# First attention: the softmax denominators' reciprocals turned once per unit, and multiplied with the gates in eight 32-row operations

## The chip, the cores and the metric

The kernel runs on one core of a Trainium2 chip. A core has five engines that run side by side: TensorE (PE, matrix products into PSUM; PEld is its loading of the stationary operand), VectorE (DVE), ScalarE (ACT), GpSimd (POOL) and SyncE (SP, which here starts most transfers). Each runs its own queue of instructions in order; semaphores hold an instruction until what it needs is there. SBUF is the memory that all read and write, PSUM (8 banks of 128x512 float32) is where PE writes. The metric is the device time of one execution in microseconds (us), the median of several runs. Engine times of single instructions are in nanoseconds (ns) where marked.

## The reference

Two layers over 256 context tokens and 1024 latent tokens of width 1024. The first is windowed attention with grouped heads and sink logits, the second latent attention. The change lies in the first: 16 heads of 64, in 4 groups that share keys and values; a block of 128 latent queries sees its own block of keys, the one before, the one behind, and the 256 context keys; a context query sees the context alone.

```
def softmax_with_sink(s, sink):
    sk = jnp.broadcast_to(sink, s.shape[:-1] + (1,))
    p = jax.nn.softmax(jnp.concatenate([s, sk], axis=-1), axis=-1)
    return p[..., :-1]
...
        p = softmax_with_sink(jnp.concatenate([s_loc, s_ctx], axis=-1), sink_b).astype(v.dtype)
        return (jnp.einsum("bhgqk,bkhd->bqhgd", p[..., :3 * BLOCK], v)
                + jnp.einsum("bhgqc,bchd->bqhgd", p[..., 3 * BLOCK:], vc))
...
    yx = (ox * jax.nn.silu(gx)) @ w_out
```

The kernel does not divide the probabilities. It multiplies the weighted values by 1/denominator and by the gate silu(g) at the end.

## The kernel before

All of it is float32; products that need the precision are split into a high and a low part (`split`, lines 272 and 273: ACT rounds to the high part, DVE or POOL subtracts for the low one) and `mm3` (lines 277 to 279) adds three products.

The first attention runs in 40 units, `UnitA(ti, g)`: a block `ti` of 128 queries (two context blocks and eight latent ones, in the order 2, 0, 3, 1, 4 to 9) and a group `g` of four heads. A unit has `m` chunks of 128 keys: 2 for a context block, 4 for the first and the last latent block, 5 for the others. Its steps:

- `score(h)`: two matmuls for each of one or two key ranges (256 context keys; up to 384 local ones) into one of three banks (`pss3`), then on DVE a fused masking, scaling and running minimum, line 696, which also writes the scores to SBUF and so frees the bank. `exp(h)` on ACT, line 702, sums the denominators.
- `T(ci)`: four transposes on PE, line 719, of the probabilities of a key chunk into a bank of the ring `pst3` (banks 6, 7, 3), then `split` (ACT, DVE) into SBUF. `PV(ci)`: two matmuls, line 729, into bank 5, accumulated over the chunks; the result has 64 + 64 rows (the two halves of the values' split) and, for each of four heads, 128 query columns.
- `post`, `post2` (lines 706 to 714): the sink's term is added to the denominators (128 queries x 4 heads, POOL), DVE takes the reciprocals (line 712), and POOL copies each head's column into 64 columns of `rb` (128x256, line 714).
- `fin`: ACT copies the halves of `PV`'s result to `o` and `o2`, laid out as 64 rows per head, two heads below each other and two side by side (128 x 2 x 128); lines 739, 740.
- `fin2`, issued in the next unit: PE transposes `rb` in two pieces of 128x128 (line 748) into a bank of `pst3`, so that row and head now match `o`. POOL adds `o2` to `o` (751), DVE multiplies the turned reciprocals by the gate `gt` into `rs` (752), POOL multiplies `o` by `rs` (753) and cuts the product in a high and a low part (755, 756) in `og`. For the last unit (`fast`) DVE does POOL's steps too.

After the four units of a block, `outproj` multiplies its `og` by the output weights; its matmuls are spread as a filler over the next block's units. DVE multiplies by the layer's gate (776), POOL adds the residual (777).

The order of instructions is not the order of the text. From the last projections of the first layer to the start of the second attention, every operation is recorded with an estimated duration and then emitted by a list scheduler (`Plan.emit`): for each engine, at the time it becomes free, the ready operation that stands earliest in the text. Its price for a DVE operation that touches PSUM is

```
        return (0.07 if psum else 0.03) + n * 0.00106, 0.37
```

with n the elements per partition, whatever the number of partitions. The banks and ring buffers are given out in the order of the text, before the scheduling.

Of the kernel before, what the change touches and what calls it, by code (L numbers as in the profile page):

```python
# [48 lines left out]
def shp(ap, *dims):  # L49
    n = 1  # L50
    for d in dims:
        n *= d
    ap = ap[:, 0:n]
    if len(dims) == 1:
        return ap
    names = "abcdefg"[: len(dims)]
    kw = {c: d for c, d in zip(names[1:], dims[1:])}
    return ap.rearrange("p (" + " ".join(names) + ") -> p " + " ".join(names), **kw)
# [151 lines left out]
def kernel(ctx: ExitStack, tc: tile.TileContext, t, out, dbg=None):  # L210
    plan = Plan()
    nc = Recorder(tc.nc, plan)
# [6 lines left out]
    F = cpool.tile([128, F_KB * KB], F32, name="arena_f")  # L219
    ident = cpool.tile([128, 128], F32, name="ident")  # L220
# [395 lines left out]
    gc = f_at(48, 1024)  # L616
    ytmp = Ring(F, [12], 512)
    wstg = Ring(F, [4, 6, 12, 34, 36], 512)
    rbr = Ring(F, [42, 47], 256)
    or1, or2, rtr = (Ring(F, [o, o - 5], 256) for o in (43, 44, 45))  # L620
    Pr = Ring(F, [14 + 2.5 * i for i in range(8)], 640)
    gr = Ring(F, [1.5, 2.5, 46], 256)
# [6 lines left out]
    pst3 = Banks(6, 7, 3)  # L629
# [15 lines left out]
    class UnitA:  # L645
# [63 lines left out]
        def post2(self):  # L709
            den = self.den  # L710
            nc.gpsimd.tensor_add(den, den, self.esk)
            nc.vector.reciprocal(den, den)
            self.rb = rbr.next()
            nc.gpsimd.tensor_copy(shp(self.rb, 4, 64), den.unsqueeze(2).to_broadcast([128, 4, 64]))

        def T(self, ci):
            pt = shp(pst3(), 4, 128)
# [25 lines left out]
        def fin2(self, fast=False):  # L743
            g, og = self.g, self.og
            o, o2 = self.o, self.o2
            rt = shp(pst3(), 4, 128)
            for j in range(2):
                nc.tensor.transpose(rt[:, j, :], self.rb[:, j * 128 : j * 128 + 128], ident)  # L748
            rs = shp(rtr.next(), 2, 128)
            eng = nc.vector if fast else nc.gpsimd  # L750
            eng.tensor_add(o, o, o2)
            nc.vector.tensor_mul(rs, rt[:, 0:2, :], self.gt)
            eng.tensor_mul(o, o, rs)
            hi = og[:, 0, 2 * g : 2 * g + 2, :]
            eng.tensor_copy(hi, o)
            eng.tensor_sub(og[:, 1, 2 * g : 2 * g + 2, :], o, hi.bitcast(F32))
# [296 lines left out]
    for bi, gp, c in order:  # L1053
# [20 lines left out]
        r = proj_t(bi, gp, c)  # L1074
# [885 lines left out]
```

## Time and profile before

| | |
|---|---|
| median of 3 runs | 1501.03 us (1500.3 to 1501.78) |
| profiled execution | 1501.05 us |
| its span, first to last instruction | 1499.2 us |
| mean granted TensorE clock | 0.998 |
| line 748 (turn of the reciprocals) | 80 transposes, 272 ns each by the profile |
| line 752 (reciprocals times gates) | 40 operations of 128x256, 421 ns each |
| line 714 (spread of the reciprocals) | 40 copies of 128x256 on POOL, 407 ns each |

How to read the profile: an engine's busy time is the time in which it executes; matmuls overlap each other, so durations of single ones add up to more than PE's time. A group is one line of the program on one engine, with output and input (partitions x elements), count, busy time, mean duration of one, and the idle time just before it with what ended it. A wait names the engine and line that waited, what it waited for, the sum, the number of times, and the longest. A timeline row gives start and duration; "x2" merges neighbours, whose duration then runs from the first one's start to the last one's end. The chain of waits goes back from the last instruction to whatever released it.

### The profile page before, as it was taken

What the parts mean: (1) busy time and instruction counts of PE and PEld (TensorE: products, weight loads), DVE (VectorE), ACT (ScalarE), POOL (GpSimd) and SP (SyncE); (2) the same over time, 40 slices, a digit from 0 to 9 for tenths busy, and PEclk for the clock granted to TensorE, in tenths of its full rate; (3) what the DMA queues carried; (4) which work ended last, traced back from release to release, by engine and by line L of the source; (5) the groups of instructions that cost most, each with busy time, mean ns of one, the idle gap of its engine ahead of it and who ended that gap; (6) DMA issues with size and microseconds to landing.
All of it is one profiled execution on the core that took longest, in us unless ns stands there. A gap on an engine that the chain in (4) does not pass through costs nothing.

```text
span 1499.2 us, 24997 instructions
## 1 busy us (share of the span) xinstructions
PE 1477.8 (99%) x9162; PEld 1201.7 (80%) x9162; DVE 954.7 (64%) x1871; ACT 709.2 (47%) x1363; POOL 820.3 (55%) x739
## 2 busy tenths in 40 slices
PE   6999999999999999999999999999999999999998
PEld 4888888888888888889888888776777767876687
DVE  4787698748778888878354004575566566566744
ACT  4421222369887888875233421453354434443322
POOL 2563365356454444457246510598788788789100
PEclk9999999999999999999999999999999999999999
DMA  9555654664354332343028622302121222121542
GB/s 338 165 175 170 204 169 155 215 205 122 115 159 127 95 102 89 94 125 132 30 85 292 195 68 85 92 15 79 47 60 54 65 59 60 48 62 30 161 148 85
DMA packets 128339, 178.93 MB, mean 119 GB/s; under 512 B 11980, under 2 KB 80716, under 8 KB 128216
## 3 DMA queue, kind: packets, MB, share of 16 engines
q1 hardware_dynamic: 123960, 170.93, 36.5%
q10 hardware_dynamic: 4256, 6.40, 1.2%
q8 instruction: 72, 1.18, 0.3%
q14 instruction: 51, 0.42, 0.1%
HBM read 131.13 MB, written 46.15 MB: 118 GB/s over the span
## 4 chain that ended last, share of the span: by engine, by line
PE 93%; DMA 2%; issue 2%; DVE 1%; POOL 1%; ACT 0%; POOLq 0%; DVEq 0%; SPq 0%; ACTq 0%
PE PB L277 15%; PE PB L278 15%; PE PB L279 15%; PE PB L1657 13%; PE PB L1680 9%; PE PB L729 5%; PE PB L1623 5%; PE PB L719 5%; PE PB L689 3%; PE PB L690 3%; DMA arena_f<-ada_w 1%; PE PB L1691 1%; PE PB L898 1%; PE PB L831 1%; PE PB L748 1%
## 5 line engine op out<-in xcount | busy, mean ns | idle before, releaser
L277 PE MATMUL PB<-arena_r 128*128 128x512 f32 (+2 forms) x1240 | 452.0, 365 | 0.0
L278 PE MATMUL PB<-arena_r 128*128 128x512 f32 (+2 forms) x1240 | 445.9, 360 | 0.4 <-DVE arena_r L273 0.3
L279 PE MATMUL PB<-arena_r 128*128 128x512 f32 (+2 forms) x1240 | 445.4, 359 | 0.0
L1673 POOL TENSOR_TENSOR arena_f<-arena_f 128x1024 f32<-128x1024 f32 x120 | 285.8, 2382 | 8.2
L277 PEld LDWEIGHTS PB<-arena_r 128*128 128x128 f32 x1240 | 233.9, 189 | 44.5 <-issue 9.2
L279 PEld LDWEIGHTS PB<-arena_r 128*128 128x128 f32 x1240 | 233.9, 189 | 34.1
L278 PEld LDWEIGHTS PB<-arena_r 128*128 128x128 f32 x1240 | 234.1, 189 | 32.9 <-DVE arena_r L273 0.7
L1657 PE MATMUL PB<-arena_r 64*128 64x512 f32 (+1 forms) x1600 | 225.8, 394 | 0.0
L1629 DVE TENSOR_REDUCE krF<-PB 128x1 f32<-128x512 f32 (+1 forms) x264 | 167.1, 677 | 78.8 <-PE PB L1623 78.8
L1667 ACT ACTIVATE arena_f<-PB 128x1024 f32<-128x1024 f32 x160 | 164.5, 1028 | 111.4 <-PE PB L1657 83.4
L273 POOL TENSOR_TENSOR arena_r<-arena_f,arena_r 128x512 fp32r<-128x512 f32 (+1 forms) x98 | 132.5, 1366 | 142.9 <-ACT arena_r L272 124.7
L273 DVE TENSOR_TENSOR arena_r<-PB,arena_r 128x512 fp32r<-128x512 f32 (+2 forms) x215 | 139.8, 662 | 76.3 <-ACT arena_r L272 75.4
L1657 PEld LDWEIGHTS PB<-arena_r 64*128 64x128 f32 (+1 forms) x1600 | 175.2, 185 | 15.8 <-issue 5.2
L696 DVE CUSTOM_DVE_ANT_0 arena_f<-PB,arena_f,small 128x256 f32<-128x256 f32 (+1 forms) x288 | 148.1, 524 | 51.4 <-PE PB L690 33.2
L272 ACT CAST arena_r<-PB 128x512 fp32r<-128x512 f32 (+2 forms) x215 | 119.9, 564 | 109.8 <-PE PB L279 73.3
L1680 PE MATMUL PB<-arena_f 128*64 128x512 f32 x640 | 145.9, 595 | 0.0
L702 ACT ACTIVATE arena_f<-arena_f,small 128x640 f32<-128x640 f32 (+2 forms) x160 | 119.1, 745 | 15.5 <-DVE small L696 13.9
L499 DVE SCALAR_TENSOR_TENSOR arena_f<-arena_f,small 128x512 f32<-128x512 f32 x98 | 113.8, 1205 | 9.9 <-DMA arena_f<-ada_w 9.5
L729 PE MATMUL PB<-arena_r 128*128 128x512 f32 x336 | 118.6, 429 | 0.0
L1623 PE MATMUL PB<-arena_r 64*128 64x512 f32 (+1 forms) x768 | 109.4, 354 | 0.0
L719 PE MATMUL PB<-ident,arena_f 128*128 128x128 f32 x672 | 108.6, 272 | 0.1
L1680 PEld LDWEIGHTS PB<-arena_f 128*64 128x64 f32 x640 | 44.0, 137 | 79.6 <-issue 78.7
(178 smaller groups left out, 1934.8 us busy)
## 6 DMA issues: line engine op xcount, KB each, us to landing
arena_f<-ada_w SPq DMA_DIRECT2D x96, 256.0 KB, 4.0
arena_r<-q_d SPq DMA_DIRECT2D x160, 128.0 KB, 2.8
arena_f<-a_w_in SPq DMA_DIRECT2D x40, 256.0 KB, 3.8
arena_f<-x SPq DMA_DIRECT2D x16, 512.0 KB, 6.6
q_d<-arena_f SPq DMA_DIRECT2D x16, 512.0 KB, 3.0
qn_d<-arena_f SPq DMA_DIRECT2D x16, 512.0 KB, 4.7
arena_r<-qn_d SPq DMA_DIRECT2D x16, 512.0 KB, 5.4
arena_f<-b_w_in SPq DMA_DIRECT2D x24, 256.0 KB, 4.7
```

The lines of the kernel that those rows point to most:

```text
L273: (lo_eng or nc.vector).tensor_sub(lo, src, hi.bitcast(F32))
L277: nc.tensor.matmul(o, ah, bh, start=first, stop=False)
L278: nc.tensor.matmul(o, al, bh, start=False, stop=False)
L279: nc.tensor.matmul(o, ah, bl, start=False, stop=last)
L719: nc.tensor.transpose(pt[:, h, :], self.Ps[h][:, ci * 128 : ci * 128 + 128], ident)
L729: nc.tensor.matmul(self.pv, V[:, self.chunks[ci], self.g, :], PT[:, s], start=ci == 0 and s == 0, stop=ci == self.m - 1 and s == 1,)
L1623: nc.tensor.matmul(bank[:, o : o + n], self.q[r, s, bs], k[r, 0, n0 : n0 + n], start=s == 0, stop=s == 2)
L1629: nc.vector.reduce_max(self.mxp[:, e, b : b + 1, i], bank[:, 0:n], AX.X)
L1657: nc.tensor.matmul(PB[:, b + e, :], k[r, s, cs], q[r, sq], start=i == 0, stop=i == 4)
L1667: nc.scalar.activation(E, PB[:, b : b + 2, :], AF.Exp)
L1673: eng.tensor_add(acc, acc, E)
L1680: nc.tensor.matmul(PB[r, 7, :], Vq[:, c, h, :], E[:, e], start=c == 0, stop=c == NT - 1)
```

## The change

`post2` spreads each head's reciprocal over 32 columns, not 64, so `rb` is 128x128 and one transpose turns it. In the turned tile, rows 32h to 32h+31 hold the reciprocals of head h. A head's 64 rows of `rs` are now made in two products of 32 rows, both from those same 32 rows of the turned tile; with four heads that is eight DVE operations of 32 partitions x 128 elements in place of one of 128 x 256. Output and gate start at partition 0, 32, 64, 96 in turn, the turned reciprocals at 32h.

```
@@ -616,7 +616,7 @@
-    rbr = Ring(F, [42, 47], 256)
+    rbr = Ring(F, [42, 47], 128)
@@ -711,7 +711,7 @@
             self.rb = rbr.next()
-            nc.gpsimd.tensor_copy(shp(self.rb, 4, 64), den.unsqueeze(2).to_broadcast([128, 4, 64]))
+            nc.gpsimd.tensor_copy(shp(self.rb, 4, 32), den.unsqueeze(2).to_broadcast([128, 4, 32]))
@@ -743,13 +743,15 @@
             o, o2 = self.o, self.o2
-            rt = shp(pst3(), 4, 128)
-            for j in range(2):
-                nc.tensor.transpose(rt[:, j, :], self.rb[:, j * 128 : j * 128 + 128], ident)
+            rt = pst3()[:, 0:128]
+            nc.tensor.transpose(rt, self.rb, ident)
             rs = shp(rtr.next(), 2, 128)
             eng = nc.vector if fast else nc.gpsimd
             eng.tensor_add(o, o, o2)
-            nc.vector.tensor_mul(rs, rt[:, 0:2, :], self.gt)
+            for h in range(4):
+                for x in range(2):
+                    r = slice(64 * (h % 2) + 32 * x, 64 * (h % 2) + 32 * x + 32)
+                    nc.vector.tensor_mul(rs[r, h // 2], rt[32 * h : 32 * h + 32], self.gt[r, h // 2])
             eng.tensor_mul(o, o, rs)
```

## The prediction

> **What bounds the kernel now.** I read the whole page first, then the stretch in which the changed lines run. Columns of the second fence are the stretch, its length, and the busy time and count of each engine.
>
> ```profile
> span 1499.2 us, 24997 instructions
> PE 1477.8 (99%) x9162; PEld 1201.7 (80%) x9162; DVE 954.7 (64%) x1871; ACT 709.2 (47%) x1363; POOL 820.3 (55%) x739
> ...
> PE   6999999999999999999999999999999999999998
> ...
> DVE  4787698748778888878354004575566566566744
> ...
> L748 PE MATMUL PB<-ident,arena_f x80: 270/272/276, 334.1 to 664.8; 128*128 128x128 f32 x80
> ```
>
> ```profile
> 340.00:655.00 315.00, 315.00 (x1932) 276.89 (x1931) 256.45 (x778) 261.76 (x644) 148.10 (x283) 1.00 0.36 108
> ...
> by line: PE PB L729 22.9%; PE PB L719 21.4%; PE PB L690 11.5%; PE PB L689 11.5%; PE PB L278 10.1%; PE PB L277 10.1%; PE PB L279 10.0%; PE PB L748 2.6%
> ```
>
> TensorE (PE) is busy nearly everywhere, and the last row of the first fence places the change: the turn of the reciprocals, line 748, runs 80 times between 334 and 665 us, in the attention stage (slices 10 to 18, where the DVE digits are 7 and 8, against 64% over the span). Between 340 and 655 us PE has no idle time, its clock is 1.00, and the chain of waits there consists of PE lines alone. DVE has 256 of 315 us, ACT 262, POOL 148. So PE sets the stage, and DVE and ACT are close behind: what counts is how much room DVE has. The waits of DVE in that stretch (total, times, longest) and its groups there:
>
> ```profile
> DVE arena_f L696 <- PE PB L690: 27.9, 44, 2.6
> DVE arena_r L273 <- ACT arena_r L272: 11.1, 24, 1.7
> DVE small L712 <- POOL small L711: 2.6, 4, 0.8
> DVE arena_f L776 <- PE PB L279: 2.5, 7, 0.4
> DVE arena_f L1113 <- POOL small L1109: 1.0, 1, 1.0
> DVE arena_f L752 <- PE PB L719: 0.5, 1, 0.5
> DVE arena_f L696 <- PE PB L719: 0.4, 1, 0.4
> ```
>
> ```profile
> L696 DVE CUSTOM_DVE_ANT_0 arena_f<-PB,arena_f,small 128x384 f32<-128x384 f32 x96 | 59.0, 615 | 9.6
> ...
> L752 DVE TENSOR_TENSOR arena_f<-PB,arena_f 128x256 f32<-128x256 f32 x37 | 15.6, 421 | 0.6 <-PE PB L719 0.5
> ```
>
> The waits sum to 46.0 us. The rest of DVE's idle time (315 - 256.5 - 46.0 = 12.5 us) is short gaps that no engine ends: 9.6 us of it stands before the second score reduction of a head, which needs the running extreme that the first one leaves, and I count it as occupied. So DVE is taken for 315 - 46 = 269 us, with 37 units in the stretch (the count of line 752), and can take 46 / 37 = 1.24 us more per unit before it is full.
>
> **The change part by part.** *PE.* One of two transposes per unit goes. The stretch's chain gives line 748 2.6% of 315 us = 8.2 us for 74 of them, 0.11 us each; 40 fewer are 4.4 us, all on the path as long as PE sets the end.
>
> *DVE.* The one product of 128x256 becomes eight of 32x128. No row shows that shape, so I take duration and pitch (start to next start) from the nearest ones.
>
> ```profile
> L386 DVE TENSOR_TENSOR krF<-PB,arena_f 128x32 f32<-128x32 f32 x8 | 1.4, 170 | 0.0
> L515 DVE TENSOR_TENSOR arena_f<-PB,arena_f 1x512 f32<-1x512 f32 x6 | 4.1, 686 | 15.2 <-PE PB L510 15.1
> L1641 DVE TENSOR_TENSOR arena_r<-PB,ident 4x512 fp32r<-4x512 f32 x32 | 22.1, 690 | 71.0 <-PE PB L1637 70.6
> L273 DVE TENSOR_TENSOR arena_r<-PB,arena_r 128x512 fp32r<-128x512 f32 x156 | 105.2, 685 | 11.5 <-ACT arena_r L272 11.1
> ```
>
> One row, 4 rows and 128 rows of 512 columns all take 686 to 690 ns: fewer rows save nothing. From 256 to 512 columns a product out of PSUM grows by 685 - 421 = 264 ns, 1.03 ns a column, so 128 columns take 421 - 132 = 289 ns (down from 256 towards the 170 ns of 32 columns, the straight line gives 278). The pitch differs between two kinds of neighbours:
>
> ```profile
> 551.58 1.28 DVE L273 TENSOR_TENSOR arena_r<-PB,arena_r 128x512 fp32r<-128x512 f32 x2
> ...
> 558.88 0.42 DVE L752 TENSOR_TENSOR arena_f<-PB,arena_f 128x256 f32<-128x256 f32 x1
> 559.21 0.47 DVE L696 CUSTOM_DVE_ANT_0 arena_f<-PB,arena_f,small 128x256 f32<-128x256 f32 x1
> ...
> 125.61 2.84 DVE L515 TENSOR_TENSOR arena_f<-PB,arena_f 1x512 f32<-1x512 f32 x4 [5.97 <-PE PB L510]
> ...
> 961.22 1.40 DVE L1641 TENSOR_TENSOR arena_r<-PB,ident 4x512 fp32r<-4x512 f32 x2 [3.71 <-PE PB L1637]
> ```
>
> Two subtractions on all 128 partitions take 1.28 us together: the second starts 1.28 - 0.685 = 0.595 us after the first, 0.09 us before that ends. Line 752 shows the same: the next instruction starts 0.33 us after it, though it lasts 0.42. Lines 515 and 1641 step over the partitions, as the new products do (rows 0, 32, 64, 96 at line 515; rows 32 and then 96 at line 1641). There the pitch is (2.84 - 0.686) / 3 = 0.72 us and 1.40 - 0.69 = 0.71: no overlap, and 0.02 to 0.03 us in between. Each of the eight products starts in another group of 32 partitions than the one before it, in its output or in an input, and the instruction behind the eighth starts at partition 0 again. So I take 289 + 30 = 0.32 us each, 2.55 us for the eight against the 0.33 of today: +2.22 us a unit. The other bound is the pitch of aligned neighbours, 289 - 90 = 0.20 us: 1.6 - 0.33 = +1.25 us a unit. I choose the first, since its rows are the ones that shift partitions.
>
> [...]
>
> Over the stretch: 37 x 2.22 = 82 us of new DVE time against 46 us of waits. If every wait were used up, DVE would need 269 + 82 = 351 us where the stage has 315: +36 us, and PE's 4.4 us are worth nothing, since PE then waits for DVE. Some waits stay. Those for PE's scores (27.9 + 0.4 + 0.5) came from PE being the slower one and should vanish; those for ACT's cast, for POOL and for the projection (11.1 + 2.6 + 2.5 + 1.0 = 17.2 us) are the order of other engines' queues. Bounds are none and all of the 17.2; I take half, 8.6, which gives +44.6 us. The other three units lie at the two ends: the opening has waits beside them, and at the closing one, 2.2 us stand on the way to the last output projection, which has other matmuls to run meanwhile. I put the ends at nothing, with 0 to 5 us as the bound.
>
> *What is behind the products.* POOL's line 753 waits for the last product and starts 2.2 us later, and behind it on POOL stand lines 755, 756 and the next unit's denominator (706, 711). The rows of POOL in the stretch:
>
> ```profile
> L753 POOL TENSOR_TENSOR arena_f<-arena_f 128x256 f32<-128x256 f32 x37 | 27.4, 741 | 19.8 <-DVE arena_f L752 19.1
> ...
> L714 POOL COPY arena_f<-small 128x256 f32<-128x256 f32 x38 | 15.5, 408 | 30.3 <-DVE small L712 20.7 <-PE PB L719 6.9 <-DVE small L1108 2.7
> ...
> L706 POOL TENSOR_TENSOR small<-small 128x4 f32<-128x4 f32 x37 | 7.6, 206 | 1.8 <-DVE small L696 1.8
> ```
>
> POOL is idle for more than half of the stretch, and a unit lasts 315 / 37 = 8.5 us, so 2.2 us of lateness does not reach the next unit's turn. The copy at line 714 halves to 128 columns, between 206 ns (4 columns) and 408: it saves at most 0.2 us a unit on POOL, worth nothing under that cover, and up to 0.2 us x 37 = 7.5 us if POOL's cover were gone. The PSUM bank of the turn, one of three shared with the transposes of line 719, is held for 2.55 us instead of 0.42; with DVE the slower engine PE has that time. No DMA is added, moved or removed, and the rings keep their places.
>
> Sum against the profiled execution, 1501.05 us with a span of 1499.2 (1.85 us lie around it; the median of the runs is 1501.03): 1501.05 + 44.6 = 1545.6, so 1546 us.
>
> **The rivals.** *DVE has room and PE stays the bound.* The products pitch at 0.20 us, fall into the 12.5 us of gaps and the waits, and the stage loses its 40 transposes: 1501 - 4.4 = 1497 us. For it: PE alone is on the chain, and 37 x 1.25 = 46 us is not above 46. Against it: it needs the aligned pitch, and every wait used to the last, without PE losing any time.
>
> *DVE is just full.* At 0.20 us DVE needs 269 + 46 = 315 us, the present length, and keeps 0 to 17 us of waits: +0 to +17, at half +9, 1510 us. For it: the aligned pairs. Against it: lines 515 and 1641.
>
> *The products cost more than their own time.* Each one held splits DVE's stream: where the written order puts other instructions between them, these lose their overlap too, 0.09 us for up to eight neighbours, 0.7 us a unit or 27 us, and the bank held longer stops PE's transposes while DVE waits for scores. +44.6 + 27 = +72, 1573 us. It decides where the eight do not run as one block. Against it: they become ready together and follow one another in the code.
>
> *PE is relieved and nothing follows,* within 3 us of before: the lower edge of the second rival, with no wait kept.
>
> **How the numbers follow.** Forecast 0.70, its own range +30 to +62 (1531 to 1563): below, the +36 less part of the short gaps; above, all 17.2 us of waits and 5 us at the ends, with a few interleaved products. First rival 0.07; DVE just full 0.13, of which 0.03 within 3 us of before; products that cost more 0.10. A measurement here can tell about 0.2%, 3 us. Faster 0.07 (the first rival); same 0.03 (the lower edge of the full-DVE case); slower 0.70 + 0.10 + 0.10 = 0.90. For 8 in 10 the range takes all of the forecast's and the upper half of the full-DVE case, and on the other side the lower part of the dearer one: 1510 to 1568.
>
> **What would show it.** In the changed profile the eight products should take about 289 ns each, a run of eight some 2.5 us; 2.2 us or less for the run with starts before the ends would mean the aligned pitch. DVE's waits in the attention stage should shrink to 5 to 20 us and its share of the stage pass 95%; PE should show idle time there, released by DVE (the score reductions of line 696 freeing PSUM, or line 273's halves), which it had none of. The last turn should come near 705 us instead of 665. If PE still has no idle time in the stage, the forecast is wrong at its root; if PE's idle time is released by POOL or ACT, the place of the bound is wrong; if the products are 0.32 us apart and the stage grows by much less than 36 us, DVE's 269 us were not as fixed as I count them.

## The result, and the profile after

The changed kernel takes 1539.64 us (median of 4 runs, 1539.14 to 1540.79) against 1501.30 us before: 38.3 us more, a ratio of 1.0255 (95% interval 1.0243 to 1.0267). The forecast was 1546 us, with 1531 to 1563 for its own case.

The page of the changed kernel, with the lines that answer to those shown of before:

```profile
span 1538.2 us, 25190 instructions
PE 1494.6 (97%) x9122; PEld 1192.4 (78%) x9122; DVE 1021.7 (66%) x2151; ACT 711.7 (46%) x1363; POOL 814.6 (53%) x739
...
DVE  3787689559999999988626102556566566566644
...
PE 77%; DVE 16%; issue 3%; DMA 1%; ACT 1%; POOL 1%; SPq 0%; DVEq 0%; POOLq 0%; ACTq 0%
```

DVE's digits in the attention stage went from 7 and 8 to 9 for most of it. The line of PE for the whole page only fell from 99% to 97%, which would tell little; the chain of waits says more, with DVE now 16% of it. The same line of the page before:

```profile
PE 93%; DMA 2%; issue 2%; DVE 1%; POOL 1%; ACT 0%; POOLq 0%; DVEq 0%; SPq 0%; ACTq 0%
```

The stage runs longer. The turn of the reciprocals (now line 747, the products line 754), then the stretch that holds about the same work as 340 to 655 us did before (156 subtractions of line 273 and 96 score reductions of 384 columns in both), and its chain:

```profile
L747 PE MATMUL PB<-ident,arena_f x40: 270/271/328, 335.9 to 705.4; 128*128 128x128 f32 x40
```

```profile
340.00:693.00 353.00, 333.56 (x1916) 271.69 (x1915) 324.12 (x1046) 265.85 (x648) 144.81 (x282) 1.00 0.32 99
```

```profile
by line: DVE arena_f L696 20.7%; DVE arena_f L754 20.7%; DVE arena_r L273 10.7%; PE PB L719 9.3%; PE PB L729 7.3%; issue 7.3%; PE PB L689 3.5%; PE PB L278 3.3%; PE PB L279 3.2%; PE PB L690 3.2%; PE PB L277 3.0%; DVE arena_f L778 1.7%; DMA a
```

The first turn starts at 335.9 us and the last at 705.4 (first and last start stand ahead of the form, behind the shortest, median and longest duration in ns); before, these were 334.1 and 664.8. From first to last turn that is 38.8 us more, and the span grew by 39.0: nearly all of the loss lies in this stage. In the stretch, PE has 19 us without work where it had none, and the chain, which was PE alone, runs through the score reductions (696), the eight products (754) and the subtractions (273). The waits of DVE there, and the two longest of PE:

```profile
DVE arena_f L754 <- PE PB L719: 6.0, 13, 0.5
DVE arena_r L273 <- ACT arena_r L272: 3.1, 5, 1.0
DVE arena_f L696 <- PE PB L690: 2.0, 6, 0.8
```

```profile
PE PB L719 <- DVE arena_f L754: 13.5, 28, 1.2
PE PB L689 <- DVE small L696: 1.5, 4, 0.5
```

DVE's waits fell from 46.0 to 11.1 us, so it is taken for 353 - 11.1 = 342 us. What it is taken by:

```profile
L754 DVE TENSOR_TENSOR arena_f<-PB,arena_f 32x128 f32<-32x128 f32 x298 | 85.2, 286 | 10.0 <-PE PB L719 6.0
```

```profile
595.27 0.87 DVE L754 TENSOR_TENSOR arena_f<-PB,arena_f 32x128 f32<-32x128 f32 x3
596.67 0.29 DVE L754 TENSOR_TENSOR arena_f<-PB,arena_f 32x128 f32<-32x128 f32 x1 [0.53 <-PE PB L719]
597.38 1.20 DVE L754 TENSOR_TENSOR arena_f<-PB,arena_f 32x128 f32<-32x128 f32 x4 [0.42 <-PE PB L719]
...
700.09 2.39 DVE L754 TENSOR_TENSOR arena_f<-PB,arena_f 32x128 f32<-32x128 f32 x8 [1.63 <-PE PB L747]
702.51 0.69 DVE L273 TENSOR_TENSOR arena_r<-PB,arena_r 128x512 fp32r<-128x512 f32 x1
```

A product takes 286 ns. A run of eight takes 2.39 us and the next instruction starts 2.42 us after it began, so a product costs 0.30 us with nothing overlapped, against 0.33 us for the whole of the old one: 2.09 us more per unit. The first three rows show something new: a run broken twice, for 0.5 and 0.4 us, by a wait for PE's transposes.

A run right behind a subtraction shows which neighbours lose the overlap:

```profile
361.31 0.69 DVE L273 TENSOR_TENSOR arena_r<-PB,arena_r 128x512 fp32r<-128x512 f32 x1
361.92 2.49 DVE L754 TENSOR_TENSOR arena_f<-PB,arena_f 32x128 f32<-32x128 f32 x8
```

The first product starts at partition 0, as the subtraction does, and 0.08 us before the subtraction ends (361.31 + 0.69 = 362.00). Behind the eighth, which starts elsewhere, the next instruction starts 0.03 us after its end (the last two rows of the fence before). So 32 rows alone do not take the overlap away.

### The profile page after: what moved, and what is told of

The parts are those of the page before. It is cut to its first block, busy times and chain, and to the rows that moved or that the text cites. A ratio compares the mean times of both kernels' runs of the same rounds, so it can differ in the third digit from the quotient of the medians.

```text
span 1538.2 us, 25190 instructions
## 1 busy us (share of the span) xinstructions
PE 1494.6 (97%) x9122; PEld 1192.4 (78%) x9122; DVE 1021.7 (66%) x2151; ACT 711.7 (46%) x1363; POOL 814.6 (53%) x739
## 4 chain that ended last, share of the span: by engine, by line
PE 77%; DVE 16%; issue 3%; DMA 1%; ACT 1%; POOL 1%; SPq 0%; DVEq 0%; POOLq 0%; ACTq 0%
PE PB L277 14%; PE PB L278 13%; PE PB L279 13%; PE PB L1659 12%; PE PB L1682 9%; DVE arena_f L696 5%; DVE arena_f L754 5%; PE PB L1625 5%; DVE arena_r L273 3%; PE PB L719 2%; PE PB L729 2%; PE PB L689 1%; PE PB L900 1%; PE PB L1693 1%; PE PB L690 1%
## 5 line engine op out<-in xcount | busy, mean ns | idle before, releaser
L719 PE MATMUL PB<-ident,arena_f 128*128 128x128 f32 x672 | 118.2, 276 | 16.5 <-DVE arena_f L754 14.4
L719 PEld LDWEIGHTS PB<-ident,arena_f 128*128 128x128 f32 x672 | 83.8, 140 | 46.8 <-DVE arena_f L754 25.1
```

Source lines behind the costliest of these rows:

```text
L719: nc.tensor.transpose(pt[:, h, :], self.Ps[h][:, ci * 128 : ci * 128 + 128], ident)
```

## The experiments

The theory under test: the stage's length is now DVE's work; a product costs 0.30 us because its start partition differs from its neighbour's; the transpose saved on PE is worth its time only while PE is the bound. All times are medians, beside runs of the kernel before on the same chip (1501.0 to 1501.7).

**The products alone** (against the kernel before, two turns kept):

```
-            nc.vector.tensor_mul(rs, rt[:, 0:2, :], self.gt)
+            for h in range(4):
+                for x in range(2):
+                    r = slice(64 * (h % 2) + 32 * x, 64 * (h % 2) + 32 * x + 32)
+                    nc.vector.tensor_mul(rs[r, h // 2], rt[r, h // 2, :], self.gt[r, h // 2])
```

> The eight 32-row products alone: two turns per unit and 64 columns per head as before, one product cut into eight. Theory DVE (the stage lasts as long as DVE's work, and PE's transposes are worth nothing while PE waits): 1539 to 1542 us, as with the change. Rival PE (the transposes count all the same): 1539.6 + 4.4 = 1544. Rival spread (32 columns per head, the shifted read in PSUM, cost the time): 1501 to 1510.

Measured: 1537.1 us, ratio 1.0240 (1.0223 to 1.0258), the change's own interval overlapping. The products alone make the whole loss, and 40 transposes more cost nothing beside them. That the products read and write the same partitions here, and cost the same (286 ns each, as with the change), takes the shifted read out of the question.

**The turn alone** (against the change):

```
-            for h in range(4):
...
+            nc.vector.tensor_mul(rs, rt.unsqueeze(1).to_broadcast([128, 2, 128]), self.gt)
```

> The single turn alone: 32 columns per head and one transpose, but one product of 128x256 as before, which takes the turned tile for both halves (so the reciprocals stand at the wrong rows). Theory DVE: PE is the bound again and the 40 transposes show in full, 1501.3 - 4.4 = 1497 us. Rival (the transposes were hidden and are worth nothing): 1501.

Measured: 1497.53 us, ratio 0.9975 (0.9965 to 0.9984). The saving is real, 3.9 us here, as long as PE sets the stage. DVE's two longest waits between 340 and 650 us show whom it waits for:

```profile
DVE arena_f L696 <- PE PB L690: 27.5, 48, 2.5
DVE arena_r L273 <- ACT arena_r L272: 7.0, 21, 1.0
```

The first is as long as before the change (27.9 us in 340 to 655): DVE waits for PE's scores, and PE has no wait in that stretch.

**Eight products that start at partition 0** (against the change):

```
-                    nc.vector.tensor_mul(rs[r, h // 2], rt[32 * h : 32 * h + 32], self.gt[r, h // 2])
...
+            spare = [F[:, int(o * KB) : int(o * KB) + 128] for o in (41, 41.5, 42.5, 47.5, 41, 41.5)]
+            for i, y in enumerate(spare + [rs[:, 0], rs[:, 1]]):
+                nc.vector.tensor_mul(y, rt, self.gt[:, i % 2])
```

> Eight products per unit with 128 columns each, but all over the 128 partitions from partition 0 (six write to spare memory, two to the place of the result; the values are not the reference's). Theory hold (a shift of the start partition takes the overlap with the neighbour away): pitch 0.20 us, the eight take 1.6 us, 1.27 more than before, and by the change's own balance (2.09 us a unit cost 38.3 us, so 45 us of 40 units' DVE time are free) 1501.3 + 51 - 45 = 1507 us, between 1499 and 1512. Rival (the duration of eight instructions sets it, wherever they start): pitch 0.30 and 1535 to 1542.

Measured: 1513.82 us, 25.8 us less than the change, and 2 us above the expected range. The group of the products, and then their row in the timeline (start, duration):

```profile
L753 DVE TENSOR_TENSOR arena_f<-PB,arena_f 128x128 f32<-128x128 f32 x320 | 68.4, 280 | 9.8 <-PE PB L719 8.2 <-PE PB L747 1.6
```

```profile
566.38 1.27 DVE L753 TENSOR_TENSOR arena_f<-PB,arena_f 128x128 f32<-128x128 f32 x6
567.57 0.68 DVE L273 TENSOR_TENSOR arena_r<-PB,arena_r 128x512 fp32r<-128x512 f32 x1
```

As many instructions with nearly the same duration (280 ns against 286), but six of them take 1.27 us: a pitch of (1.27 - 0.28) / 5 = 0.20 us instead of 0.30, and the next one starts 0.08 us before the sixth ends. 0.10 us x 320 = 32 us of DVE's time and 25.8 us of the kernel's hang on where an instruction starts.

**Fewer and more products** (against the change): four (`for x in range(1)`), six (`for x in range(2 if h < 2 else 1)`), and each made twice (`for h in (0, 1, 2, 3, 0, 1, 2, 3)`).

> The change with four of the eight products left out (the second 32 rows of each head are not multiplied). Theory DVE (0.30 us a product; 45 us of the 40 units' DVE time are free, beyond that the time grows one to one): 4 x 0.30 - 0.33 = 0.87 us a unit, 35 us, under the 45: PE is the bound again, 1497 us, up to 1502. Rival line (each product adds its share of the 38.3 us): 1501 + 0.87 / 2.09 x 38.3 = 1517.

> Two of the eight left out (the second 32 rows of heads 2 and 3). Theory DVE: 6 x 0.30 - 0.33 = 1.47 us a unit, 59 us against 45 free: +14, 1515 us, 1508 to 1520. Rival line: 1501 + 1.47 / 2.09 x 38.3 = 1528.

> Each of the eight products made twice. Theory DVE: 16 x 0.30 - 0.33 = 4.5 us a unit, 180 us against 45 free: +134, 1635 us, 1625 to 1645. Rival line: 1501 + 4.5 / 2.09 x 38.3 = 1584.

Measured, beside the run with one turn and one product as the start (new DVE time is (products x 0.30 - 0.33) x 40; for sixteen, 0.317 takes the place of 0.30, see below):

| products per unit | new DVE time, us | kernel, us | ratio to before (interval) | grown by, per us of new DVE time |
|---|---|---|---|---|
| 1 (the old one) | 0 | 1497.5 | 0.9975 (0.9965 to 0.9984) | |
| 4 | 35 | 1504.8 | 1.0026 (1.0015 to 1.0036) | 7.3 / 35 = 0.21 |
| 6 | 59 | 1518.7 | 1.0117 (1.0102 to 1.0132) | 13.9 / 24 = 0.58 |
| 8 (the change) | 83 | 1539.6 | 1.0255 (1.0243 to 1.0267) | 20.9 / 24 = 0.87 |
| 16 | 190 | 1644.5 | 1.0956 (1.0940 to 1.0973) | 105 / 107 = 0.98 |

The theory had the time flat up to 45 us of new work and one to one beyond; the rival had one slope throughout. Both are off: there is a bend, but it is soft. Four products came out 3 us above the theory's range and far below the rival's 1517; six inside it; sixteen at its upper edge, which the rival (1584) misses by 60 us.

With sixteen, the products stood further apart than 0.30 us. A run of fifteen in that profile:

```profile
371.66 4.75 DVE L754 TENSOR_TENSOR arena_f<-PB,arena_f 32x128 f32<-32x128 f32 x15
```

At 0.287 us for the last one that is a pitch of (4.75 - 0.287) / 14 = 0.319 us; the median over the profile is 0.317. With it, the theory's rule gives 1501 + 190 - 45 = 1646 us. Why the gaps are longer here is open.

The run from partition 0 lies on the same curve: its (8 x 0.20 - 0.33) x 40 = 51 us would give 1514 us on a straight line between four and six products, and it took 1513.8. So the start partition counts through the DVE time it costs.

**Four products of 64 rows, two turns kept** (against the kernel before):

```
-            nc.vector.tensor_mul(rs, rt[:, 0:2, :], self.gt)
+            for h in range(4):
+                r = slice(64 * (h % 2), 64 * (h % 2) + 64)
+                nc.vector.tensor_mul(rs[r, h // 2], rt[r, h // 2, :], self.gt[r, h // 2])
```

> Two turns as before, the product cut into four of 64 rows x 128. Theory DVE: 4 x 0.30 - 0.33 = 0.87 us a unit, under what is free: 1501 to 1506 us. Rival line: 1517.

Measured: 1506.04 us, ratio 1.0033 (1.0020 to 1.0045). A product lasts 287 ns here with 64 rows, 286 with 32 and 280 with 128: the rows don't enter. The time is at the upper end of the theory's range, and 1.3 us above the four products with a single turn.

**The bank freed early** (against the change):

```
-                    nc.vector.tensor_mul(rs[r, h // 2], rt[32 * h : 32 * h + 32], self.gt[r, h // 2])
+                    nc.vector.tensor_mul(rs[r, h // 2], rt[0:32] if h + x == 0 else ident[r], self.gt[r, h // 2])
```

> Only the first of the eight products reads the turned tile in PSUM; the other seven read the identity in SBUF at the same rows as the gate (so the values are not the reference's). The PSUM bank is free 2 us earlier, DVE's work stays. Theory DVE: 1531 to 1541 us; the waits in the middle of the eight go (some 6 us). Rival bank (the ring of three banks, held by the products, stops PE): at or below 1515.

Measured: 1551.54 us, outside both. The two longest waits of PE in 340 to 650 us, the products, and the spread of their durations (shortest, median, longest in ns):

```profile
PE PB L689 <- DVE small L696: 11.4, 19, 2.2
PE PB L719 <- DVE arena_r L273: 8.0, 10, 1.7
```

```profile
L754 DVE TENSOR_TENSOR arena_f<-ident,arena_f 32x128 f32<-32x128 f32 x280 | 102.9, 368 | 8.1 <-DMA g_d<-arena_f 1.6 <-ACT arena_f L702 1.0 <-POOL arena_f L755 0.2
L754 DVE TENSOR_TENSOR arena_f<-PB,arena_f 32x128 f32<-32x128 f32 x40 | 10.9, 273 | 0.2
```

```profile
L754 DVE TENSOR_TENSOR arena_f<-ident,arena_f x280: 248/284/1358, 309.5 to 706.5; 32x128 f32<-32x128 f32 x140
```

The wait for line 754 is gone, as intended, and so are the breaks in the run by line 719; PE waits for other work of DVE instead, and the time did not fall. So the held bank alone is not what costs. But the edit did not keep DVE's work as it was: the products with two operands in SBUF took 368 ns on the mean, 102.9 + 10.9 - 320 x 0.286 = 22 us more in all, of which the kernel shows 11.9. The median is still 284 ns. In the trace, 50 of the 280 took more than 400 ns, each of them while POOL was executing, and the 122 that met no instruction of POOL took 284 ns on the mean; with the turned tile in PSUM as one operand, none of the change's 320 took more than 299. The bank and the breaks in the run may therefore be worth up to some 10 us of the 38.3; this run can't say how much.

**The scheduler's price** (against the change):

```
-        return (0.07 if psum else 0.03) + n * 0.00106, 0.37
+        return (0.17 if out.shape[0] == 32 else 0.07 if psum else 0.03) + n * 0.00106, 0.37
```

> The change with the scheduler's price of a 32-row DVE operation raised by 0.1 us to the measured 0.30, so that the written order allows for it. Theory DVE: the work stays, 1530 to 1541 us. Rival order (the order, laid for cheaper products, costs the time): below 1520.

Measured: 1531.86 us, 7.8 us below the change. Its two longest waits of PE, 340 to 650 us:

```profile
PE PB L689 <- DVE small L696: 2.7, 5, 1.1
PE PB L719 <- DVE arena_f L754: 2.2, 6, 0.7
```

An order laid out for the true price gives back a fifth of the loss, and PE's wait for the products' bank shrinks from 12.3 us in that window with the change to 2.2. The other 30 us stay.

**Half of the units**, in the hope of a version that beats both (against the kernel before; odd groups take the new form), then the same with the raised price:

```
+            n = 32 if self.g % 2 else 64
+            nc.gpsimd.tensor_copy(shp(self.rb, 4, n), den.unsqueeze(2).to_broadcast([128, 4, n]))
...
+            for j in range(1 if g % 2 else 2):
...
+            if g % 2:
...
+            else:
+                nc.vector.tensor_mul(rs, rt[:, 0:2, :], self.gt)
```

> The change in every second unit only (odd groups), the old form in the others. Theory DVE: 20 x 2.09 = 42 us of new DVE time against 45 free, and 20 transposes fewer: at best 1501.3 - 2.2 = 1499 us, 1499 to 1504 with some waits. Rival line: 1501 + 19 = 1520.

> The change in every second unit, as in the run before that gave 1516 us, with the scheduler's price of a 32-row operation raised by 0.1 us. Theory order (the 14.5 us came from an order laid for cheaper products): 1499 to 1505. Rival lumps (DVE's free time lies in small pieces, a few tenths of a us before each unit's scores, and a run of 2.4 us in one unit can't use that of the other): 1509 to 1516.

Measured: 1515.99 us, ratio 1.0096 (1.0081 to 1.0111), and with the raised price 1511.31 us, ratio 1.0066 (1.0053 to 1.0079). The theory missed the first by 12 us. The order accounts for 4.7 us of it. The bend in the table accounts for more: as an estimate, 42 us of new work give about 1509 us there, and the 20 transposes that stay some 2 us on top. DVE's waits in the first one, 340 to 650 us:

```profile
DVE arena_f L696 <- PE PB L690: 10.4, 23, 2.3
DVE arena_r L273 <- ACT arena_r L272: 8.4, 19, 1.1
```

About 19 us of waiting are left unused in these two rows while the stage is already longer: DVE's idle time can't be spent wherever it is wanted. That it is the lumps, 2.4 us of products in one unit out of reach of the idle time of the next, fits the second run's range, but was not tried by itself, and with the raised price little is left for it beyond the table's 1511.

**The turn by DMA** (against the kernel before): no transpose, no copy, the product on POOL.

```
+            d = rec_d[4 * self.ti + self.g]
+            load(out=d.rearrange("h q -> q h"), in_=den)
...
+                load(out=self.rb[64 * e : 64 * e + 64], in_=src.partition_broadcast(64))
...
+            eng.tensor_mul(rs, self.rb, self.gt)
```

> Neither form: the reciprocals (128x4) go to DRAM turned (4x128) and come back spread over 64 rows per head by two broadcast loads; no transpose and no copy per unit, and the product with the gate runs on POOL (SBUF alone), not on DVE. Theory DVE and PE: PE loses 80 transposes of 0.11 us (8.8 us), DVE loses one product a unit, POOL gains 0.34 us a unit of its idle time: 1501.3 - 8.8 = 1492.5 us. Rival late (two transfers one after the other, 3 to 5 us each by the loads of the profile, and SyncE's queue held behind the reciprocals, make the products late and og and the queries' loads with them): 1501 or more.

Measured: 1718.46 us, ratio 1.1444 (1.1428 to 1.1460). The longest waits, 340 to 650 us, of SyncE's queue and of the engines:

```profile
SPq L720 <- DMA rec_d<-small: 131.2, 18, 10.5
```

```profile
POOL arena_f L755 <- DMA arena_f<-rec_d: 135.1, 17, 11.7
DVE small L713 <- POOL small L712: 88.8, 20, 10.7
```

The broadcast load waits 131.2 / 18 = 7.3 us in SyncE's queue until the 128x4 values have landed, POOL then waits 8 us a time for it, and the next unit's denominators stand behind that on POOL. That is the rival's mechanism; its "1501 or more" named no price, and it costs 217 us. No version that makes the whole product with the reciprocals at their rows beats the kernel before.

## Why the prediction was right

**PE is the bound before, and loses that place.** Shown: the turn alone gives 3.9 us (forecast 4.4), and beside the eight products it gives nothing (1537.1 with two turns, 1539.6 with one).

**The price of a product.** Forecast 289 ns and 0.32 us from one to the next, measured 286 ns and 0.30. The choice between the two pitches was what decided: at the aligned pitch the forecast's second rival said 1510, and the run with eight products from partition 0 gave 1513.8. (In that aligned case 1.6 - 0.33 is 1.27 us a unit and not the 1.25 of the recorded sum, so its new work is 47 us and not 46; the choice does not hang on it.) What the runs show of the two pitches: with the change, a product that follows another without a wait starts in another group of 32 partitions than that one, and it starts 13 to 32 ns after that one's end (261 pairs in the trace). The product at 361.92 us and the subtraction ahead of it, which both start at partition 0, overlap by 0.08 us, and so do the last of the products from partition 0 and the subtraction behind them. The rows 0.30 and 0.20 us apart, with nearly the same duration (286 and 280 ns), put the difference at 0.10 us a product here.

**DVE's balance.** Forecast was 269 + 82 = 351 us of taken time in the stretch; measured 342, 73 more than before. The pitch accounts for 5 of the 9 us (37 x (2.22 - 2.09) = 4.8); the rest does not lie in the short gaps, which came to 353 - 324.1 - 11.1 = 17.8 us after 12.5. Other instructions of DVE took less from one start to the next (waits left out): the 156 subtractions 606 ns by the trace, after 627, which is 3.3 us. Fewer of them now stand before idle time of DVE, where nothing overlaps their end (3 by the trace, after 39); that this is the reason was not tested.

**The waits that stay.** Forecast 8.6 us, left by ACT, POOL and the projection; measured 11.1, but not the ones named. POOL's and the projection's are gone, ACT's fell from 11.1 to 3.1 us, 2.0 us for PE's scores stayed that were to vanish, and 6.0 us are new: the products wait for PE's transposes in the middle of their run. That half of the 17.2 us came near the measured sum is luck. The prediction had the bank down as held longer with time to spare; that the transposes and the products would stop each other in turn was not in it; nor that PE's idle time would end mostly with line 754 (13.5 us), where the forecast named lines 696 and 273. Why the runs break there is not shown; with seven of the eight products reading SBUF the breaks were gone.

**The ends.** Forecast nothing: the first turn starts 1.8 us later, and what follows the last one takes 1.6 us less (40.6 us against 39.0).

So the forecast's 44.6 us against 38.3: the mechanism was right, and the term that was too large is DVE's new time, 82 us for 73. POOL's lateness and the halved copy had no part that any run showed, as forecast; neither was tried by itself.

**What did not hold** is a finer point: the 46 us of waits were treated as a store that is used up first and one to one beyond. The row of 1, 4, 6, 8 and 16 products shows 0.21, 0.58, 0.87 and 0.98 us per us of new work, and the half version lost 14.5 us with waits left. For the change itself the difference is small, since it lies far enough above the bend.

## What to carry to other kernels

Where PE has no idle time and DVE is taken for 85% of a stage (269 of 315 us), a trade of PE time for DVE time must be priced per unit against DVE's waits per unit: here 0.11 us was bought for 2.09 us where 1.24 us were free. Price a vector operation by count and columns, not by rows (here it took 280 to 287 ns for 128 columns on 32, 64 or 128 rows, and 421 ns for 256 columns), and look in the trace for a pair with the same kind of neighbour: here operations that hop over the partitions cost 0.30 us apiece where aligned ones of as many columns cost 0.20. Idle time of the second engine is not a store: 35 us of new work where about 50 were free (46 / 37 x 40) already cost 7.3 us.

## What the runs showed that was not expected

The granted TensorE clock was below 1.00 in the two runs in which PE was kept waiting most. Between 340 and 650 us (the columns are PE, PEld, DVE, ACT, POOL, clock, DMA share, GB/s), in the run with sixteen products and in the one with the turn by DMA:

```profile
340.00:650.00 310.00, 257.05 (x1293) 203.71 (x1293) 279.94 (x923) 181.15 (x448) 100.86 (x198) 0.91 0.27 82
```

```profile
340.00:650.00 310.00, 223.97 (x1108) 188.26 (x1108) 144.98 (x441) 155.02 (x395) 107.33 (x188) 0.84 0.40 86
```

At 83% and 72% of busy time the clock is 0.91 and 0.84; with the change, at 333.56 / 353 = 94%, it stays at 1.00. Why it is lower there is not shown. What the lower clock costs was not separated; the time with sixteen products leaves little to it, at 0.98 us per us of new work.
